# In what pieces the last output blocks of a gated MLP leave, and from which step

## The chip, the cores and the metric

The kernel runs on one core of a Trainium2 chip. The metric is the device time of one execution in microseconds (us). TensorE (PE) multiplies, ScalarE (ACT) and VectorE (DVE) take results out of PSUM, GpSimd (POOL) adds tiles and starts some transfers, and SyncE (SP) computes nothing: it starts DMA transfers. DMA transfers started by SP run on the queue that the profile calls q1, those started by ACT on q10; both are carried by the same 16 DMA engines.

## The reference

```python
# x: 16 x 256 x 512, w1: 512 x 4096, w2: 2048 x 512, all float32
h = x @ w1
gate, value = np.split(h, 2, axis=-1)
h = np.maximum(gate, 0) * value
return (h @ w2).astype(np.float32)
```

With the two leading axes of `x` taken together there are 4096 rows of 512.

## The kernel before

The rows are worked on in four sets (`s` = 0 to 3) of 1024. Both products are computed by a scheme of Strassen's kind: each is cut into 2 x 2 quarters, and seven products, `P1` to `P7`, of sums of quarters take the place of eight. The inputs are cast to float16; sums collect in float32 in PSUM.

The first product of a set runs in 16 blocks of 128 hidden columns (`class Block`). The second product of a set is a generator, `mm2_stream(s, go)`. Its matmuls are slipped in, four at a time, between those of the next set's first product, so that TensorE always has work; the last set's stream (`last`, `s` = 3) has nothing to hide behind and runs alone at the end of the program.

Within `mm2_stream` an output block `b` (0 to 3) stands for 128 rows of the set's upper half and 128 of the lower. Each of the seven products of a block is a chain of eight matmuls (`mm`, L288 to L293; the profile's L291), and each has its own evacuation in `step`:

- `P2`: ACT writes the left half of the upper output tile `o1` (L315).
- `P3`: DVE writes the right half of `o1` (L321), and SP sends `o1` to DRAM (L324). In the last set the blocks with `b` >= 1 go as two halves of 256 columns, 128 KB each; all others go whole, 256 KB.
- `P7`: DVE writes the right half of the lower output tile `o2` (L327). In the last set SP sends this half at once for the last block, `b` = 3 (L330).
- `P4`: ACT writes the left half of `o2` (L333). For `b` = 3 of the last set ACT itself sends this half (L335, on its own queue). In every other case SP sends the whole `o2` (L337).

`o2` is a part of the buffer named `pv`, so in the profile `out_dram<-pv` are the lower blocks and `out_dram<-o` the upper ones.

The order of the steps is written out by hand (`order`, L340 to L343). It ends with P6 of b=2 and 3, P3 of b=2 and 3, P7 of b=2 and 3, P4 of b=2 and 3. Every engine runs its instructions in the order in which they are recorded, so SP's last transfers before the change are: `o1` of b=2 in two halves, `o1` of b=3 in two halves, the right half of `o2` of b=3 (L330), the whole `o2` of b=2 (L337). Then come the program's branch (L45: the results of a test of the inputs decide whether a general way must be run as well; it is not run here) and the closing semaphore instructions (the launch line, L648), in which SP waits for every transfer that is still out.

A transfer that SP or ACT starts also waits until the transfer eight places before it, on the same semaphore, has landed.

Of the kernel before, what the change touches and what calls it, by code (L numbers as in the profile page):

```python
# [25 lines left out]
HALF = 256  # L26
# [3 lines left out]
@with_exitstack  # L30
def kernel(ctx: ExitStack, tc: tile.TileContext, x, w1, w2, out):

    nc = tc.nc
    x2 = x.flatten_outer_dims()
    out2 = out.flatten_outer_dims()  # L40
    flagpool = ctx.enter_context(tc.tile_pool(name="flagpool", bufs=1))
    flag = flagpool.tile([1, 1], dt.int32, name="flag")
    with ExitStack() as fast:
        unfit = fast_way(fast, tc, x2, w1, w2, out2, flag)
    with tc.If(unfit > 0, label="general"):  # L45
        with ExitStack() as general:
            general_way(general, tc, x2, w1, w2, out2)
# [52 lines left out]
def fast_way(ctx, tc, x2, w1, w2, out2, flag):  # L100

    nc = tc.nc
    T, D = x2.shape
    _, J = w1.shape
    H, DO = w2.shape
# [4 lines left out]
    NB = TH // P  # L110
# [11 lines left out]
    w1_v = w1.rearrange("(e p) (g j) -> p e g j", p=P, g=2)  # L122
    w2_v = w2.rearrange("(hc p) n -> p hc n", p=P)
    x_v = x2.rearrange("(s b p) d -> s p b d", p=P, b=2 * NB)
    out_v = out2.rearrange("(s h b p) n -> s h b p n", p=P, b=NB, h=2)
# [43 lines left out]
    gate = wpool.tile([P, 1], F32, name="gate")  # L169

    first = wpool.tile([P, 4], F32, name="first")
    nc.scalar.dma_start(out=first[:128], in_=w1_v[:128, :, 0, 0])

    def idle(n):
        for _ in range(n):
# [108 lines left out]
    def mm2_stream(s, go):  # L284
        last = s == NS - 1
        S = {}

        def mm(name, b, ps, fresh):  # L288
            vn, gn = WX[name]
            for k in range(NHC):  # L290
                nc.tensor.matmul(ps, go[gn][:, k, b * P:(b + 1) * P], V[vn][:, k, :], start=fresh and k == 0,  # L291
                                 stop=k == NHC - 1, skip_group_check=True)
                if k < NHC - 1:  # L293
                    yield

        def take(pool, nm):
            return pool.tile([P, TH], F32, name=nm, tag=nm)[:, :HALF]

        def step(name, b):
            d = S.setdefault(b, {})  # L300
            if name == "P1":
                d["X"] = take(psx, "X")
                yield from mm("P1", b, d["X"], True)
                d["Y"] = take(psy, "Y")
                nc.scalar.copy(out=d["Y"], in_=d["X"])
            elif name == "P5":
                d["W"] = take(psw, "W")
                yield from mm("P5", b, d["W"], True)
                t = tmp.tile([P, 2, TH], F32, name="pv", tag="tmp")
                d["pu"], d["o2"] = t[:, 0].rearrange("p (a n) -> p a n", a=2), t[:, 1]  # L310
                nc.scalar.activation(d["pu"][:, 0], d["W"], COPY, scale=1 / GS)
            elif name == "P2":
                yield from mm("P2", b, d["X"], False)
                d["o1"] = tmp.tile([P, DO], F32, name="o", tag="o", bufs=4)
                nc.scalar.activation(d["o1"][:, :HALF], d["X"], COPY, scale=1 / GS)  # L315
            elif name == "P6":
                yield from mm("P6", b, d["Y"], False)
                nc.scalar.activation(d["pu"][:, 1], d["Y"], COPY, scale=-1 / GS)
            elif name == "P3":
                yield from mm("P3", b, d["W"], False)  # L320
                nc.vector.scalar_tensor_tensor(out=d["o1"][:, HALF:], in0=d["W"], scalar=1 / GS, in1=d["pu"][:, 1],  # L321
                                               op0=MULT, op1=ADD)
                for n in (slice(0, HALF), slice(HALF, DO)) if last and b else (slice(0, DO),):
                    nc.sync.dma_start(out=out_v[s, 0, b, :, n], in_=d["o1"][:, n])  # L324
            elif name == "P7":
                yield from mm("P7", b, d["Y"], False)
                nc.vector.scalar_tensor_tensor(out=d["o2"][:, HALF:], in0=d["Y"], scalar=-1 / GS, in1=d["pu"][:, 0],  # L327
                                               op0=MULT, op1=ADD)
                if last and b == NB - 1:
                    nc.sync.dma_start(out=out_v[s, 1, b, :, HALF:], in_=d["o2"][:, HALF:])  # L330
            else:
                yield from mm("P4", b, d["Y"], False)
                nc.scalar.activation(d["o2"][:, :HALF], d["Y"], COPY, scale=1 / GS)  # L333
                if last and b == NB - 1:
                    nc.scalar.dma_start(out=out_v[s, 1, b, :, :HALF], in_=d["o2"][:, :HALF])  # L335
                else:
                    nc.sync.dma_start(out=out_v[s, 1, b], in_=d["o2"])  # L337
            yield

        order = [("P1", 0), ("P1", 1), ("P1", 2), ("P2", 0), ("P2", 1), ("P2", 2)]  # L340
        order += [(n, b) for n in ("P5", "P6", "P3", "P7", "P4") for b in (0, 1)]
        order += [("P1", 3), ("P5", 2), ("P2", 3), ("P5", 3)]
        order += [(n, b) for n in ("P6", "P3", "P7", "P4") for b in (2, 3)]  # L343
        for i, (n, b) in enumerate(order):
            for f in BESIDE.get((s, i), ()):
                f()
            yield from step(n, b)
# [190 lines left out]
    for s in range(NS):  # L538
        if s:
            g, go = g_tiles()  # L540
        first = NPLAIN if s == 0 else 0
# [4 lines left out]
        last = NJ * PERIOD  # L546
# [16 lines left out]
        for at in range(first * PERIOD, last + PERIOD):  # L563
            if at in plan:
                jb, n = plan[at]
# [87 lines left out]
```

## Time and profile before

| | us |
|---|---|
| median of 4 runs (309.27 to 309.72) | 309.66 |
| the profiled execution | 309.57 |
| its span, first to last instruction | 307.8 |
| PE busy | 300.1 |
| DVE busy | 219.3 |
| ACT busy | 189.7 |
| last ACT evacuation (L333, b=3) starts, ends | 303.00, 303.38 |
| last transfer (L335) is started | 303.42 |

The granted TensorE clock is 0.997 over the span. The page's row of HBM traffic:

```profile
HBM read 24.12 MB, written 11.53 MB: 116 GB/s over the span
```

How to read the views used below. The page gives the busy time of each engine and the chain of work that ended last. A timeline row gives start, duration, engine, source line, operation, the tile written and the tiles read; `SPq` and `ACTq` are the instructions with which SP and ACT start a transfer, and their duration is that of the start alone. The DMA view counts, for a stretch of time, the packets and megabytes of each DMA queue and the time their packets took as a share of 16 engines: 100% would be all sixteen engines moving that queue's packets for the whole stretch. A 256 KB output of 128 rows is 128 packets of 2 KB, eight on each engine, and 16 more of a few bytes that mark completion, one on each engine; a half block is 128 packets of 1 KB and the 16 marks. Queues with the kind "instruction" carry the engines' own program.

### The profile page before, as it was taken

To read this page: it belongs to the slowest core of one execution; us is meant where nothing else is said; L and a number is where in the kernel's file an instruction comes from. 1 tells how busy PE (TensorE), PEld (TensorE's weight loads), DVE (VectorE), ACT (ScalarE), POOL (GpSimd) and SP (SyncE) were. 2 spreads that over 40 slices of the span, in tenths; PEclk is the share of its full clock that TensorE was granted. 3 is DMA by queue.
4 is the path that set the end of the run, shared out by engine and by line. 5 is a ranking of instruction groups with operands and counts; after the bars stand their busy time and mean duration, and the time that the engine had idled before them with its cause. 6 is when DMAs were issued, how large, how long until landed. Compare 5 with 4: busy or idle time off the path is not lost.

```text
span 307.8 us, 5116 instructions
## 1 busy us (share of the span) xinstructions
PE 300.1 (97%) x1868; PEld 181.9 (59%) x1868; DVE 219.3 (71%) x346; ACT 189.7 (62%) x457; POOL 139.7 (45%) x127
## 2 busy tenths in 40 slices
PE   7899999999999999999999999999999999999993
PEld 3574444588844444488864444458884444448883
DVE  1798898896468888884338888886526888888311
ACT  2557776568577676738766767656856767673230
POOL 1749999810004438980002245994000343998000
PEclk9999999999999999999999999999999999999998
DMA  6999986989615740064130010037321100000223
GB/s 225 306 204 205 209 209 181 187 151 196 230 58 102 139 102 1 2 129 146 70 137 27 8 34 2 0 69 140 140 91 45 34 11 25 0 2 0 70 90 120
DMA packets 34410, 31.54 MB, mean 102 GB/s; under 512 B 14448, under 2 KB 28784, under 8 KB 34160
## 3 DMA queue, kind: packets, MB, share of 16 engines
q1 hardware_dynamic: 24608, 20.32, 21.8%
q0 software_dynamic: 9104, 10.75, 21.2%
q8 instruction: 15, 0.25, 0.3%
q10 hardware_dynamic: 672, 0.13, 0.2%
q14 instruction: 11, 0.09, 0.1%
HBM read 24.12 MB, written 11.53 MB: 116 GB/s over the span
## 4 chain that ended last, share of the span: by engine, by line
PE 95%; DMA 2%; ACT 0%; SPq 0%; issue 0%; ACTq 0%
PE Y L205 26%; PE X L205 17%; PE W L205 17%; PE Y L291 14%; PE W L291 9%; PE X L291 9%; DMA g<-in_w_dram 2%; PE W L255 2%; PE X L255 1%; PE Y L255 1%; SPq L418 0%; PE X L390 0%; ACT Y L212 0%; ACT wr L400 0%; ACT pv L333 0%
## 5 line engine op out<-in xcount | busy, mean ns | idle before, releaser
L280 POOL TENSOR_TENSOR g_S<-g 128x512 f16<-128x512 f16 (+1 forms) x46 | 58.1, 1292 | 126.2 <-DVE g L244 126.2
L205 PEld LDWEIGHTS <-wt 128*128 128x128 f16 x488 | 47.7, 98 | 55.9 <-issue 0.3
L205 PE MATMUL X<-x_A,wr 128*128 128x512 f16 x244 | 72.6, 379 | 0.1
L205 PE MATMUL Y<-x_S,wt 128*128 128x512 f16 x244 | 72.6, 379 | 0.0
L205 PEld LDWEIGHTS <-wr 128*128 128x128 f16 x366 | 35.8, 98 | 41.5 <-issue 0.4
L232 DVE SCALAR_TENSOR_TENSOR cc<-W,pu 128x512 f32<-128x512 f32 x61 | 42.2, 692 | 24.1 <-ACT pu L226 24.1
L212 ACT COPY Y<-X 128x512 f32<-128x512 f32 x61 | 34.8, 570 | 38.0 <-PE X L205 37.6
L291 PEld LDWEIGHTS <-g_S 128*128 128x128 f16 x512 | 50.0, 98 | 5.8
L238 DVE SCALAR_TENSOR_TENSOR cc<-Y,pu 128x512 f32<-128x512 f32 x61 | 42.2, 691 | 6.3
L226 ACT ACTIVATE pu<-Y 128x512 f32<-128x512 f32 x61 | 36.4, 596 | 13.9 <-PE Y L205 13.9
L233 DVE SCALAR_TENSOR_TENSOR g<-X,cc 128x512 f16<-128x512 f32 x61 | 42.2, 692 | 2.4
L244 DVE SCALAR_TENSOR_TENSOR g<-Y,cc 128x512 f16<-128x512 f32 x61 | 41.6, 681 | 1.8 <-PE Y L205 1.8
L291 PEld LDWEIGHTS <-g 128*128 128x128 f16 x384 | 37.5, 98 | 8.2
L219 ACT ACTIVATE pu<-W 128x512 f32<-128x512 f32 x61 | 36.8, 603 | 0.3 <-PE W L205 0.3
L205 PE MATMUL W<-x_S,wt 128*128 128x512 f16 x122 | 36.3, 379 | 0.0
L205 PE MATMUL W<-x_S,wr 128*128 128x512 f16 x122 | 36.3, 379 | 0.0
L205 PE MATMUL Y<-x_A,wt 128*128 128x512 f16 x122 | 36.3, 379 | 0.0
L291 PE MATMUL X<-w,g 128*128 128x256 f16 x256 | 31.2, 273 | 0.0
L291 PE MATMUL Y<-v,g_S 128*128 128x256 f16 x256 | 30.6, 273 | 0.0
L321 DVE SCALAR_TENSOR_TENSOR o<-W,pv 128x256 f32<-128x256 f32 x16 | 6.8, 424 | 29.8 <-PE W L291 29.8
L280 POOL TENSOR_TENSOR g_S<-g,g_S 128x512 f16<-128x512 f16 x18 | 21.8, 1209 | 1.4
L280 POOL TENSOR_TENSOR g_S<-g_S,g 128x512 f16<-128x512 f16 x18 | 20.8, 1155 | 1.4
(76 smaller groups left out, 284.6 us busy)
## 6 DMA issues: line engine op xcount, KB each, us to landing
out_dram<-pv SPq DMA_DIRECT2D x15, 256.0 KB, 2.0
out_dram<-o SPq DMA_DIRECT2D x13, 256.0 KB, 2.1
x<-in_x_dram POOLq DMA_DIRECT2D x3, 1024.0 KB, 8.1
xn<-x SPq DMA_DIRECT2D x12, 256.0 KB, 3.2
g_S<-in_x_dram SPq DMA_DIRECT2D x4, 512.0 KB, 6.5
wr<-in_w_dram POOLq DMA_DIRECT2D x4, 512.0 KB, 12.9
w<-in_w_dram POOLq DMA_DIRECT2D x4, 512.0 KB, 15.2
g<-in_w_dram SPq DMA_DIRECT2D x2, 512.0 KB, 6.6
```

What stands on the lines that cost most here:

```text
L205: nc.tensor.matmul(ps, W(wn, self.jb)[:, b], self.xo[xn][:, b, :], start=fresh and b == 0, stop=b == 1, skip_group_check=True)
L212: nc.scalar.copy(out=self.Y, in_=self.X)
L219: nc.scalar.activation(self.p5, self.W, COPY, scale=GS)
L226: nc.scalar.activation(self.u2, self.Y, COPY, scale=-GS)
L232: nc.vector.scalar_tensor_tensor(out=self.c12, in0=self.W, scalar=GS, in1=self.u2, op0=MULT, op1=ADD)
L233: nc.vector.scalar_tensor_tensor(out=self.g[:, self.jb, :TH], in0=self.X, scalar=0.0, in1=self.c12, op0=MAX, op1=MULT)
L238: nc.vector.scalar_tensor_tensor(out=self.c22, in0=self.Y, scalar=-GS, in1=self.p5, op0=MULT, op1=ADD)
L244: nc.vector.scalar_tensor_tensor(out=self.g[:, self.jb, TH:], in0=self.Y, scalar=0.0, in1=self.c22, op0=MAX, op1=MULT)
L255: nc.tensor.matmul(ps[:, ts], W(names[e // 2], self.jb)[:, e % 2], self.a[:, e, ts], start=e == 0, stop=e == 3, skip_group_check=True)
L280: eng.tensor_tensor(go[n][:, h0:h1], go[i0][:, h0:h1], go[i1][:, h0:h1], op=op)
L291: nc.tensor.matmul(ps, go[gn][:, k, b * P:(b + 1) * P], V[vn][:, k, :], start=fresh and k == 0, stop=k == NHC - 1, skip_group_check=True)
L321: nc.vector.scalar_tensor_tensor(out=d["o1"][:, HALF:], in0=d["W"], scalar=1 / GS, in1=d["pu"][:, 1], op0=MULT, op1=ADD)
```

## The change

For the last set only, the blocks are cut at other places:

- upper blocks (`P3`, L324): b=1 goes whole instead of in two halves; b=2 and b=3 go in halves as before.
- lower blocks: for b=2 too the right half is sent behind P7 (L330), and behind P4 only the left half is sent, 128 KB instead of 256 KB, still by SP. b=3 is as before.
- the load of one column of `w1` into `first` is written without the slice `:128`; the tile has 128 rows.

The count of transfers stays the same: one fewer for `o1` of b=1, one more for `o2` of b=2. SP's last transfers are now: `o1` of b=2 in two halves, `o1` of b=3 in two halves, the right half of `o2` of b=2, the right half of `o2` of b=3, the left half of `o2` of b=2. The instructions of PE, DVE, ACT and POOL are the same, in the same order.

```diff
-    nc.scalar.dma_start(out=first[:128], in_=w1_v[:128, :, 0, 0])
+    nc.scalar.dma_start(out=first, in_=w1_v[:, :, 0, 0])
...
-                for n in (slice(0, HALF), slice(HALF, DO)) if last and b else (slice(0, DO),):
+                for n in (slice(0, HALF), slice(HALF, DO)) if last and b >= 2 else (slice(0, DO),):
                     nc.sync.dma_start(out=out_v[s, 0, b, :, n], in_=d["o1"][:, n])
...
-                if last and b == NB - 1:
+                if last and b >= NB - 2:
                     nc.sync.dma_start(out=out_v[s, 1, b, :, HALF:], in_=d["o2"][:, HALF:])
...
                 if last and b == NB - 1:
                     nc.scalar.dma_start(out=out_v[s, 1, b, :, :HALF], in_=d["o2"][:, :HALF])
                 else:
-                    nc.sync.dma_start(out=out_v[s, 1, b], in_=d["o2"])
+                    n = slice(0, HALF if last and b == NB - 2 else DO)
+                    nc.sync.dma_start(out=out_v[s, 1, b, :, n], in_=d["o2"][:, n])
```

## The prediction

> **What bounds the kernel now.** I read the page first, then the chain of waits at the end, the timeline of the last microseconds, and the DMA view in narrow windows. The page says that TensorE is the whole kernel:
>
> ```profile
> PE 300.1 (97%) x1868; PEld 181.9 (59%) x1868; DVE 219.3 (71%) x346; ACT 189.7 (62%) x457; POOL 139.7 (45%) x127
> PE 95%; DMA 2%; ACT 0%; SPq 0%; issue 0%; ACTq 0%
> ```
>
> PE is busy for 300.1 of 307.8 us. The edit touches no matmul, and no DVE or ACT operation, so the only time it can change is the stretch behind the last matmul. The timeline of that stretch:
>
> ```profile
> 300.39 0.42 DVE L327 SCALAR_TENSOR_TENSOR pv<-Y,pv 128x256 f32<-128x256 f32 x1 [0.39 <-PE Y L291]
> 301.26 0.42 DVE L327 SCALAR_TENSOR_TENSOR pv<-Y,pv 128x256 f32<-128x256 f32 x1 [0.45 <-PE Y L291]
> 301.71 0.33 SPq L330 DMA_DIRECT2D out_dram<-pv  x1
> 302.13 0.38 ACT L333 ACTIVATE pv<-Y 128x256 f32<-128x256 f32 x1 [3.98 <-PE Y L291]
> 302.54 0.33 SPq L337 DMA_DIRECT2D out_dram<-pv  x1
> 303.00 0.38 ACT L333 ACTIVATE pv<-Y 128x256 f32<-128x256 f32 x1 [0.49 <-PE Y L291]
> 303.42 0.38 ACTq L335 DMA_DIRECT2D out_dram<-pv  x1
> ```
>
> The two DVE rows are P7 of b=2 and of b=3. L330 sends the right half of b=3, L337 the whole of b=2 (256 KB), L335 the left half of b=3 (128 KB). In the DMA views the times from issue to landing are 2.5 us for L330, 3.2 for L337 and 2.7 for L335, so they land at 304.2, 305.7 and 306.1. The span ends at 307.8: some 1.7 us of closing semaphore instructions (L648) that start when L335 has landed. So **the landing of L335 sets the end**, and its issue, behind the last ACT copy, is not moved by the edit. It takes 2.7 us, where the other 128 KB outputs of the page take 1.8 (median of six). The edit can only win from the 0.9 us between.
>
> What holds L335 back shows in three windows of the DMA view: 303.0 to 304.25, 304.65 to 305.26, and 305.26 to 305.62.
>
> ```profile
> q8 instruction: 1, 0.02, 6.1%
> ...
> q10 hardware_dynamic: 41, 0.03, 14.7%
> q1 hardware_dynamic: 6, 0.01, 6.5%
> ...
> q10 hardware_dynamic: 9, 0.01, 6.5%
> q1 hardware_dynamic: 1, 0.00, 0.2%
> ```
>
> q1 is SP's queue and q10 ACT's. In the first window one single packet of instructions (0.02 MB) takes 6.1% of 16 engines over 1.25 us: 0.061 x 16 x 1.25 = 1.22 us on one DMA engine, from 303.0 to 304.2. In the second window L337 still has six packets to go, and in the third, behind the very last packet of q1 (its completion mark), come exactly nine packets of q10: 144 packets / 16 engines = 9, one engine's whole share of L335 (eight of data and the mark). So one DMA engine, call it X, was held by the instruction load to 304.2, then moved its eight 2 KB packets of L337 until 305.26, and only then began its share of L335, until 305.62; 0.5 us later that is seen as landed.
>
> **The change, part by part.**
>
> The load of `first` (L172) is written differently and is the same transfer: 0. So is the slice of L337 for every other block.
>
> P3 of b=1: its two halves (L324) become one transfer. SP loses one DMA and one wait. The three issues of L324 (b=0, then the two halves of b=1) stand in the timeline from 288.47 to 289.79, so the right half goes out at about 289.4, and with it now the whole. SP next stands still at L337 of b=0 until 292.1, and nothing reads an output. Even at 5.1 us, the longest landing of any output, it is down by 294.5, 11 us before the end: 0, hidden by 13 us of matmuls.
>
> P7 of b=2: SP gains one DMA, L330 for b=2. DVE is done at 300.39 + 0.42 = 300.81; SP starts L330 0.03 us after DVE, as it does for b=3 (301.68 to 301.71), so at 300.84, and is free at 301.17. Behind it in SP's queue stand L330 of b=3, which cannot go before 301.71, and the send of b=2 behind P4, not before 302.54: 0.54 us of slack, then 0.50. Cost on the path: 0. Its packets should run some 0.83 us after the start of the issue (L330 now: 301.71, first packets at 302.54), so from 301.67 to 302.2. That stretch is empty now: the window from 301.5 to 302.45 shows no packet at all.
>
> P4 of b=2: 128 KB instead of 256 KB leave at 302.54. This is the part that can gain. On engine X eight packets of 1 KB take the place of eight of 2 KB. Two rows price it.
>
> ```profile
> q1 hardware_dynamic: 145, 0.26, 74.5%
> ...
> q1 hardware_dynamic: 432, 0.39, 73.9%
> ...
> q1 hardware_dynamic: 9, 0.01, 6.9%
> ```
>
> First, the plain pace. The window 292.8 to 293.75 holds one 256 KB output: 0.745 x 16 x 0.95 / 128 = 0.088 us per 2 KB packet. The window 299.9 to 301.5 holds three of 128 KB: 0.739 x 16 x 1.6 / 384 = 0.049 us per 1 KB packet. Eight of each: 0.71 against 0.39, a gain of 0.31. Second, a like case: an instruction load of the same 0.02 MB at 290.6 leaves one engine working alone on 1 KB packets, and in the window from 291.745 to 292.466 that engine moves exactly eight of them and a mark, in 0.72 us. L337's share took 305.26 - 304.22 = 1.04 us. Gain 1.04 - 0.72 = 0.32. I take **0.32**, the second, because it has the load in front of it as the path does. Bounds: 0 below (the load, or another engine, holds L335 whatever L337 weighs), 0.9 above (L335 lands in the undisturbed 1.8 us).
>
> A rule speaks against counting on this. The Trainium skill, "Runtime: NRT & Kernel Launch", section "Instruction fetch mechanics", says that instructions come in blocks of 16 KiB and that a taken branch out of the window forces such a load. The load on q8 agrees with it in size, but the other queue of instructions, q14, shows 0.01 MB and 5.6% of 16 engines over the 0.65 us from 304.05, which is 0.58 us. With a full block there (an estimate, 1.2 us as on q8) it would run to 305.3 and L335 behind it to 305.7, so no gain, 309.6; by the row it is gone at 304.7.
>
> The sum is made against the profiled execution: 309.57 (span 307.8 and 1.8 around it) - 0.32 = 309.25. That execution is 0.09 under the median of the runs, 309.66, which gives 309.34; I say **309.3**.
>
> **Rivals.**
>
> *Nothing moves (25%).* L335 is held by something else: the engine that is last but one. The window from 305.1 on shows ten packets of q10, X's nine and a single one more, so that engine ends some 0.5 us before X; if it too is held by an instruction load (q14 at 304.1, on an engine no view names), it may slip later. For it: two loads fall into this stretch. Against: nine q10 packets stand in a row behind q1's last mark. Time 309.6.
>
> *L335 lands undisturbed (12%).* Its landing falls from 2.7 to 1.8 us: 309.57 - 0.9 = 308.7. For it: with half the bytes the other fifteen engines are free before L335 comes. Against: the load on q8 follows TensorE's branch (L45 at 301.8), which the edit does not move, so X is still taken until 304.2 and owes 0.72 + 0.39 us of work after that.
>
> *Slower, through SP's queue (8%).* The added L330 stands in front of L330 of b=3 and of the P4 send. Issues are 0.33 us as a rule, but the longest L324 took 1.06. Two such: 300.84 + 2.12 = 302.96 instead of 302.54, so the P4 send and SP's own branch come 0.42 us late. It decides once the two issues together take over 1.70 us. The price: SP's instruction load then comes at 304.5 instead of 304.1, and on X it would stand before L335: 305.62 - 0.32 + 0.58 = 305.88, 0.26 over now: 309.8. Against: from 150 us on no output's issue on SP takes over 0.40.
>
> **How the numbers follow.** 55% for the forecast. The range, 308.9 to 309.8, holds the forecast, no movement and the third rival at its price, over eight in ten; the undisturbed landing lies outside. A difference under 0.2% (0.62 us) cannot be told from no change here, and 0.32 us is half of that. Faster by more needs a landing gain of over 0.62 us: most of the second rival and a little of the forecast's tail, 0.15. Slower by more would need over twice the third rival's price: 0.05. The rest, 0.80.
>
> **What would show it.** L330 twice, at 300.8 and 301.7, each 0.33 us. Packets on q1 from about 301.7 to 302.2. The P4 send of b=2 at 302.5 landing in about 2.9 instead of 3.2 us, L335 in about 2.4. The last q10 packet at about 305.3 instead of 305.6, and the closing instructions still 1.7 us. PE busy as before, 300 us. Wrong it would be if L335 still takes 2.7 us (another holder), if it takes 1.8, or if the closing stretch behind the last landing changes length.

## The result, and the profile after

| | runs | median us | range | 
|---|---|---|---|
| before | 78 | 309.80 | 309.12 to 311.51 |
| changed | 52 | 309.34 | 308.79 to 311.98 |

The ratio is 0.9981, with a 95% interval of 0.9972 to 0.9990: some 0.6 us faster by the ratio, 0.46 us by the medians, just at the border of what this kernel can show.

The profiled execution of the changed kernel, though, is a late one: 310.83 us, with a span of 308.9 us against 307.8. So the two traces must be compared stretch by stretch. First the page, span and engines:

```profile
span 308.9 us, 5116 instructions
PE 302.3 (98%) x1868; PEld 184.0 (60%) x1868; DVE 219.4 (71%) x346; ACT 189.5 (61%) x457; POOL 139.6 (45%) x127
```

PE is busy for 2.2 us more, with the same 1868 matmuls. Where that came from shows at the very start. Here is PE's timeline of the changed kernel, and then that of the kernel before (start, duration, what):

```profile
1.28 3.59 PE L177 MATMUL Y<-warm 128*128 128x512 f16 x8 [1.28 <-DVE warm L167]
5.58 1.94 PE L383 MATMUL W<-ident,g_S 128*128 128x128 f32 x8 [0.70 <-DMA g_S<-in_x_dram]
```

```profile
1.28 3.60 PE L177 MATMUL Y<-warm 128*128 128x512 f16 x8 [1.28 <-DVE warm L167]
5.51 1.06 PE L382 MATMUL W<-ident,g_S 128*128 128x128 f32 x8 [0.64 <-DMA g_S<-in_x_dram]
```

The eight warming matmuls are alike, but the first eight transposes, the same work, take 1.94 us instead of 1.06. The trace's record of the granted clock begins its stretch at full speed at 10.28 us in the changed kernel and at 5.47 in the kernel before. From some 14 us on each matmul runs 1.45 us later. Of what the edit touches only the load of `first` has run by then; its issue takes 476 ns from 0.8 us on in both traces, and it lands after 4.3 us before and 4.4 now. This is a lottery of the first microseconds that both kernels play (below).

What the edit does lies at the other end. The timeline there, of SP and of ACT:

```profile
302.29 1.21 SPq L330 DMA_DIRECT2D out_dram<-pv  x2
303.99 0.33 SPq L338 DMA_DIRECT2D out_dram<-pv  x1
...
303.58 0.38 ACT L333 ACTIVATE pv<-Y 128x256 f32<-128x256 f32 x1 [3.98 <-PE Y L291]
304.45 0.38 ACT L333 ACTIVATE pv<-Y 128x256 f32<-128x256 f32 x1 [0.49 <-PE Y L291]
304.87 0.38 ACTq L335 DMA_DIRECT2D out_dram<-pv  x1
```

L330 now stands there twice (the first at 302.29, less the 1.45 us at 300.84, as forecast), and L338 is the send behind P4. To take out the late start I count from the start of the last ACT evacuation: 303.00 before, 304.45 now. To the span's end it was 4.78 us and is 4.48: **0.30 us shorter**. L335 lands 2.4 us after its issue instead of 2.7; here are its rows in the DMA views, before and now:

```profile
out_dram<-pv ACTq DMA_DIRECT2D x1, 128.0 KB, 2.7
out_dram<-pv ACTq DMA_DIRECT2D x1, 128.0 KB, 2.4
```

The DMA view shows how, in three windows: 304.44 to 305.70, 305.68 to 306.418 and 306.415 to 306.8.

```profile
q8 instruction: 1, 0.02, 6.1%
...
q1 hardware_dynamic: 9, 0.01, 6.9%
...
q10 hardware_dynamic: 9, 0.01, 6.1%
```

The instruction load on q8 ends at 305.69 (0.061 x 16 x 1.26 = 1.23 us long, as before). Then the engine that it held moves L338's eight 1 KB packets and the mark, until 306.41: 0.72 us, where eight of 2 KB took 1.04. Last come the nine packets of q10, its share of L335, until 306.76.

### The profile page after: what moved, and what is told of

Its sections match the earlier page's. It is cut to its first block, busy times and chain, and to the rows that moved or that the text cites. A ratio compares the mean times of both kernels' runs of the same rounds, so it can differ in the third digit from the quotient of the medians.

```text
span 308.9 us, 5116 instructions
## 1 busy us (share of the span) xinstructions
PE 302.3 (98%) x1868; PEld 184.0 (60%) x1868; DVE 219.4 (71%) x346; ACT 189.5 (61%) x457; POOL 139.6 (45%) x127
## 4 chain that ended last, share of the span: by engine, by line
PE 96%; DMA 1%; ACT 0%; issue 0%; SPq 0%; ACTq 0%
PE Y L205 25%; PE X L205 17%; PE W L205 17%; PE Y L291 14%; PE X L291 9%; PE W L291 9%; PE W L255 2%; DMA g_S<-in_x_dram 1%; PE X L255 1%; PE W L383 1%; PE Y L255 1%; PE X L383 1%; PE X L391 0%; ACT Y L212 0%; PE Y L177 0%
```

## The experiments

Each run's trace gives the same few marks. They are read from its DMA and instruction records, in us from the start of the last ACT evacuation (L333): when the load on q8 ends, when q1's last packet ends, the difference of these two, when q10's last packet ends, when L335 has landed, when the span ends, and the closing stretch, which is the last minus the one before it (taken before rounding).

| kernel | KB behind P4 | load ends | q1 ends | difference | q10 ends | L335 landed | span ends | closing |
|---|---|---|---|---|---|---|---|---|
| before | 256 | 1.23 | 2.27 | 1.04 | 2.61 | 3.07 | 4.78 | 1.70 |
| changed | 128 | 1.24 | 1.96 | 0.72 | 2.31 | 2.78 | 4.48 | 1.70 |
| e1 P7, P4 part alone | 128 | 1.35 | 2.08 | 0.72 | 2.42 | 2.89 | 5.64 | 2.75 |
| e2 P3 part alone | 256 | 1.22 | 2.26 | 1.03 | 2.60 | 3.06 | 4.84 | 1.77 |
| e3 right half twice | 256 | 0.88 | 1.92 | 1.04 | 2.26 | 2.72 | 4.43 | 1.70 |
| e4 left half unsent | 0 | 0.87 | | | 1.81 | 2.16 | 3.93 | 1.77 |
| e5 no general way | 128 | no load | 0.89 | | 1.79 | 2.14 | 3.10 | 0.96 |
| e6 late branch | 128 | 3.15 | 1.00 | | 3.87 | 4.36 | 6.06 | 1.70 |
| e7 nine warming | 128 | 1.08 | 1.80 | 0.72 | 2.15 | 2.62 | 4.32 | 1.70 |
| e8 four warming | 128 | 0.85 | 1.58 | 0.72 | 2.00 | 2.46 | 4.16 | 1.70 |
| e10 b=0 in halves | 256 | 1.08 | 2.12 | 1.03 | 2.46 | 2.92 | 5.68 | 2.75 |
| e11 b=2 whole | 128 | 0.99 | 1.70 | 0.71 | 2.04 | 2.51 | 4.71 | 2.20 |
| e12 before, nine | 256 | 0.99 | 2.02 | 1.03 | 2.37 | 2.83 | 4.53 | 1.70 |
| e13 changed, nine | 128 | 1.00 | 1.72 | 0.72 | 2.06 | 2.54 | 4.24 | 1.70 |

### e1 and e2: one part of the change at a time

```diff
 e1, against the changed kernel
-    if last and b >= 2 else (slice(0, DO),):      # L323, P3
+    if last and b else (slice(0, DO),):
 e2, against the kernel before
-    if last and b else (slice(0, DO),):           # L323, P3
+    if last and b >= 2 else (slice(0, DO),):
```

> The change without its P3 part: b=1 of the upper blocks goes in two halves again, only the P7 and P4 sends of b=2 are changed. Theory (the gain is the halved send of b=2 behind P4, on the one DMA engine that the instruction load of TensorE holds): the stretch from the start of the last ACT evacuation to the span's end is as in the changed kernel, 4.48 us (before: 4.78), and L335 takes 2.4 us to land; time some 0.3 us under the kernel before. Rival (the whole block of b=1 does it): the stretch is 4.78 and L335 takes 2.7.

> Of the change only the P3 part: b=1 of the upper blocks goes whole, the lower block of b=2 goes whole behind P4 as before. Theory: nothing moves, last stretch 4.78 us, L335 takes 2.7 us, the same time as the kernel before within 0.1%. Rival: the stretch is 4.48 and 0.3 us are won.

e1: 310.28 us median against 309.83 of the kernel before beside it, ratio 1.0018 [0.9994, 1.0042]. e2: 309.98, ratio 0.9996 [0.9972, 1.0021]. e2 came as expected but for 0.07 us in the closing stretch. e1 is a miss: L335 lands as the theory wants (2.5 us, with a load that took 1.37 us instead of 1.23), but the span ends 5.64 us after the last evacuation began, not 4.48. **The split alone makes the kernel slower**; the P3 part, priced at nothing, is what saves it. The interval of all the times still takes in 1, because late starts widen both groups; the trace shows it (5.64 us against 4.78 before), and among the runs under 310.5 us, which I take to be the early starts, e1 has a median of 310.22 and the kernel before beside it 309.74.

What SP waits for at the end shows the reason. The view of SP's waits gives who waited for whom, total us, times, longest. First the changed kernel, then e1:

```profile
SPq L45 <- SPq L45: 2.5, 4, 1.5
```

```profile
SPq L45 <- SPq L45: 2.9, 1, 2.9
```

And the rows of L45 and of L649's drains by source line (durations least, median, most in ns; first and last start), again the changed kernel and then e1:

```profile
L45 SPq EVENT_SEMAPHORE  x8: 17/17/17, 304.9 to 307.2; - x8
...
L649 SPq DRAIN  x3: 7/13/36, 308.1 to 308.6; - x3
```

```profile
L45 SPq EVENT_SEMAPHORE  x8: 17/17/17, 305.8 to 306.4; - x8
...
L649 SPq DRAIN  x3: 7/7/136, 307.6 to 308.0; - x3
```

Behind its branch, and under the branch's line L45, SP waits for the eight DMA semaphores one after the other, in the same order in every trace that has the branch. In the changed kernel it passes six early, stands 1.5 us at the seventh (L338), and the last of the eight is L335's: the others lie in the shadow of the landings. In e1 there is one transfer more, and since transfers take the eight semaphores in turn, L335 gets the next one round, the *first* that SP asks for. SP stands there for 2.9 us, and seven more waits follow behind the landing, from 305.82 to 306.37: 0.54 us. (e2 fits: with one transfer fewer L335 falls on the seventh, one wait is left behind it, and the closing stretch is 0.07 us longer.) A second piece lies inside L649, and the view of waits has no row for it. By the start times in the instruction records SP stands for 0.36 us in front of its first drain, where the changed kernel has 0.04, and the drain takes 136 ns instead of 13; with three waits before it that came a little slower, L649 takes 2.13 us from its first instruction to the span's end instead of 1.62, 0.51 us more. 0.54 + 0.51 is the 1.05 us by which the closing stretch grew.

### e10 and e11: the count of transfers, without the split and with it

```diff
 e10, against the kernel before
-    if last and b else (slice(0, DO),):           # P3
+    if last else (slice(0, DO),):
 e11, against the changed kernel
-    if last and b >= 2 else (slice(0, DO),):      # P3
+    if last and b % 2 else (slice(0, DO),):
```

> The kernel before with b=0 of the upper blocks in halves too: one more transfer of 128 KB, at about 288 us, 15 us before the end, and nothing else. In the kernel without the P3 part the eight closing waits of SP (L45) all came after L335 had landed, since L335 then uses the semaphore that SP waits for first, and the closing stretch behind its landing grew from 1.70 to 2.75 us. Theory (the number of transfers decides which of eight semaphores L335 uses, and so whether SP's other closing waits lie in its shadow): the closing stretch behind the landing is 2.7 us here too, the whole stretch from the last ACT evacuation about 5.8 us, the time about 1.0 us over the kernel before. Rival (it was the early send of b=2): as the kernel before, 1.71 and 4.78 us.

> The changed kernel with another upper block left whole: b=1 goes in halves again and b=2 whole, so that the number of transfers is that of the changed kernel. Theory (the P3 part is there to keep the count, whichever block pays): closing stretch 1.70 us, the stretch from the last ACT evacuation 4.1 to 4.6 us according to how long TensorE's instruction load takes, the time as the changed kernel. Rival (b=1 itself must go whole): closing stretch 2.7 us, 1 us slower.

e10: 310.65 us against 309.74, ratio 1.0042 [1.0025, 1.0059]; closing stretch 2.75 us. One more transfer of a block that left 15 us before the end costs 0.9 us, with nothing of the split in it (4.78 to 5.68 us; the load happened to be 0.15 us shorter). That is shown as the theory said.

e11: 309.94 us, ratio 1.0010 [0.9996, 1.0024]; closing stretch 2.20 us. This is half a miss, and a useful one. The count of transfers is that of the changed kernel and L335 is again on the semaphore asked for last, so the 0.54 us of waits are gone. But the other 0.5 us is still there: L649 again takes 2.12 us to the span's end instead of 1.62. SP stands for 0.37 us in front of its second drain, and that drain is a long one:

```profile
L649 SPq DRAIN  x3: 7/13/131, 306.5 to 307.2; - x3
```

So it is a cost of its own. It goes with how many *instructions* SP has run. A transfer that waits for two things needs an instruction more than one that waits for one; the left half of b=2, which SP sends by itself in the changed kernel, needed only the one, and in e11 it goes with the whole block. Counted in the traces, SP runs 150 instructions in both kernels, 152 in e1 and e10 and 151 in e11, and in these three the stop comes at the 148th each time (the first closing drain in e1 and e10, the second in e11). In the kernels with 150 the 148th is a wait for GpSimd: in the changed kernel SP passes it 0.22 us behind ACT, but GpSimd is still clearing semaphores then and the end is no later for it. In e2 and e4, with 148, it is the last instruction of all. That SP fetches its next block of program there is my reading of a place that stays fixed while instructions move past it. The DMA records speak for it: the last 8 KB load on q14, one of the queues that carry program, begins 0.64 to 0.65 us behind the start of the 148th instruction in eleven of the thirteen traces with the branch (0.57 in e2, 0.71 in e6), wherever that instruction stands. But it begins when the stop is over, so it is not what SP stood for, and what was is not shown.

### e3 and e4: the bytes behind P4

```diff
 e3, against the changed kernel
+                elif last and b == NB - 2:
+                    spare = dpool.tile([P, DO], F32, name="spare")
+                    nc.sync.dma_start(out=spare[:, HALF:], in_=d["o2"][:, HALF:])
...
-                    n = slice(0, HALF if last and b == NB - 2 else DO)
+                    n = slice(0, DO)
 e4, against the changed kernel
-                else:
+                elif not (last and b == NB - 2):
```

> The changed kernel, but the early right half of b=2 goes to a spare buffer in DRAM, and behind P4 the whole block of b=2 goes, 256 KB. The same number of transfers behind P7, the old bytes behind P4. Theory (bytes in front of L335 decide): stretch back at 4.78 us, L335 2.7 us, the send behind P4 3.2 us. Rival (what counts is that something leaves early, or the order of the transfers): 4.48 us and 2.4.

> The changed kernel without the send of the left half of b=2 behind P4: that half block is left out of the output. Theory: the held engine has nothing in front of its share of L335 but the instruction load, so it begins when the load ends (1.25 us after the start of the last ACT evacuation) and moves its eight packets in 0.72 us; L335 lands 2.0 us after its issue, stretch about 4.1 us. Rival (another engine, the last but one, holds L335 next): L335 still lands at 1.9 to 2.4 us and the stretch stays between 4.1 and 4.48.

e3: 309.49 us against 309.83, ratio 0.9982 [0.9965, 0.9999]; 4.43 us. By its time this is a miss: as fast as the changed kernel, with the old bytes behind P4. By the trace the bytes do what the theory says and something else moved. The load on q8, in the window from 304.43 to 305.33:

```profile
q8 instruction: 1, 0.02, 6.1%
```

That is 0.061 x 16 x 0.90 = 0.88 us instead of 1.23, and behind it the 2 KB packets took 1.04 us, as in every trace with 256 KB. With a load of 1.22 us, as before, its 4.43 would be 4.77 (an estimate). Whether this program's load is short in all its runs or was so in the profiled one cannot be told from the times alone, so e3 by itself does not decide; the table's column of differences does. It reads 1.03 or 1.04 in all five traces with 256 KB and 0.71 or 0.72 in all six with 128 KB where the load stands in front, whenever the load ended (0.85 to 1.35 us).

e4, which leaves that half block out of the output: 308.86 us, ratio 0.9961 [0.9943, 0.9980]; 3.93 us, where 4.1 was expected, again with a load of only 0.88 us; it ends before L335's data come out, and L335 lands in 1.7 us, as undisturbed. The closing stretch is 1.77 us, as in e2: here too there is one transfer fewer.

### e5 and e6: the load itself

```diff
 e5, against the changed kernel
-    with tc.If(unfit > 0, label="general"):
-        with ExitStack() as general:
-            general_way(general, tc, x2, w1, w2, out2)
...
-    BESIDE[NS - 1, 20] = [lambda: tc.mark_branch_hint_location(
-        "general", engines=[ENG.PE, ENG.SP, ENG.Activation, ENG.DVE, ENG.Pool])]
 e6, against the changed kernel, behind L335's line
+                    nc.tensor.matmul(take(psw, "W")[:1, :1], d["o2"][:, :1], d["o2"][:, :1], start=True, stop=True)
```

> The changed kernel without the general way and the branch to it (the fast way's result and its test of the inputs are as before; the way for unfit inputs is left out). Theory: without the branch no engine loads instructions from a far place at the end, so no packet on q8 or q14 in the last 5 us, no engine is held, L335 lands in the undisturbed 1.8 us, and the stretch behind the start of the last ACT evacuation is some 0.6 us shorter than in the changed kernel, 3.9 us. Rival (L335 is slow because of what runs on q1 in front of it, loads or not): L335 still takes 2.4 us and the stretch stays at 4.48 less what the branch itself costs.

> The changed kernel with one more matmul of 1 x 1 at the very end that reads what the last ACT evacuation wrote; TensorE so reaches its branch about 1.6 us later (303.4 in place of 301.8 on the clock of the kernel before). Theory: the load on q8 starts 1.25 us after that branch, so some 0.35 us after the first packets of L335, when most of them are through; the engine that it holds has moved its share, L335 lands in 1.9 to 2.0 us, the stretch is about 4.05 us, 0.4 us under the changed kernel. Rival (the load is not what holds L335): 4.48 us, or longer by the matmul.

e5: 307.62 us, ratio 0.9908 [0.9873, 0.9943]; 3.10 us. The DMA view from 301 to the end has no queue of instructions left:

```profile
q1 hardware_dynamic: 568, 0.52, 30.0%
q10 hardware_dynamic: 144, 0.13, 7.6%
...
out_dram<-pv ACTq DMA_DIRECT2D x1, 128.0 KB, 1.7
```

L335 lands in 1.7 us; together with e4 that says that the loads are what held it: 0.64 us of the 1.38 by which e5's stretch is shorter. The rest, 0.74 us, is closing stretch (0.96 instead of 1.70), which the theory had not counted. It is no version to use, since unfit inputs would get a wrong result.

e6: 310.93 us, ratio 1.0037 [1.0013, 1.0061]; 6.06 us. A miss, and my mechanism for the load's timing falls with it. TensorE's branch came 1.68 us later, as meant, and of the loads behind the branches only that on q8 came later with it, so it is TensorE's. But it did not start 1.25 us behind it, where L335 would mostly have been through; it started 1.84 us behind it, at 305.18, and L335 was *not* through. In the windows from 305.18 to 306.06 and from 306.04 to 306.8:

```profile
q8 instruction: 1, 0.02, 6.2%
...
q10 hardware_dynamic: 9, 0.01, 6.7%
```

A whole engine's share of L335, nine packets, moved only behind the load, though the other fifteen engines were done with theirs some 0.3 us before the load's packet begins, and from 304.92 to 305.18 no packet moved at all. So the engine is taken for longer than the load's own packet shows. Why, and from when, stays open. The order is the same as before the edit: load first, outputs behind it.

### e7, e8, e12 and e13: the start

```diff
 e7 and e13, against the changed kernel; e12, against the kernel before
-NWARM = 8
+NWARM = 9
 e8, against the changed kernel
-NWARM = 8
+NWARM = 4
```

> The changed kernel with nine warming matmuls instead of eight at the start, so that TensorE idles some 0.2 us instead of 0.6 to 0.7 before the first transposes. In the profile of the changed kernel the granted clock reaches full speed only at 10.28 us, in that of the kernel before at 5.47, and everything up to the last set lies 1.45 us later. Theory (the clock's rise is decided by how long TensorE idled in the first microseconds, and the two groups of times, near 309.4 and near 311, are the two cases): the group near 311 vanishes, all times lie under 309.9, the median is some 0.3 us lower or the same. Rival (the late rise has another cause): the group stays at a sixth to a third of the runs.

> The changed kernel with four warming matmuls instead of eight: TensorE idles some 2.3 us before the first transposes. Theory (as for nine): every run has the late rise of the clock, all times near 310.8 to 311.3, and the profile shows full speed after 8 us. Rival (the first set's start does not depend on the warming): two groups as in the changed kernel, median near 309.4.

> The kernel before with nine warming matmuls. Theory: no run with the late rise of the clock, so all times between 309.1 and 310.1, median about 309.6.

> The changed kernel with nine warming matmuls, beside the kernel before with nine on the same chip: the change's own size without the lottery of the first microseconds. Theory: 0.3 us under that kernel, median about 309.25, all times under 309.9. Rival (part of the measured gain was that fewer of its runs began late): the two are within 0.1 us.

| kernel | warming matmuls | runs | over 310.5 us | median us | ratio to before |
|---|---|---|---|---|---|
| before (with the changed kernel) | 8 | 78 | 23 | 309.80 | |
| changed | 8 | 52 | 5 | 309.34 | 0.9981 [0.9972, 0.9990] |
| e8 changed | 4 | 10 | 7, all over 310.3 | 310.89 | 1.0017 [0.9997, 1.0038] |
| e7 changed | 9 | 12 | 0 | 309.24 | 0.9975 [0.9958, 0.9992] |
| e12 before | 9 | 12 | 0 | 309.50 | 0.9996 [0.9985, 1.0006] |
| e13 changed | 9 | 12 | 0 | 309.25 | 0.9977 [0.9963, 0.9990] |

With four, the first eight transposes take 1.94 us again and the clock's record reaches full speed at 9.52 us. With nine no run of 36 was late. The theory's result holds, its mechanism does not quite: in e7's trace TensorE still idles 0.73 us before the first transposes, since the clock had already risen at 4.2 us and the nine matmuls took only 3.54.

```profile
1.28 3.54 PE L177 MATMUL Y<-warm 128*128 128x512 f16 x9 [1.28 <-DVE warm L167]
5.55 1.06 PE L383 MATMUL W<-ident,g_S 128*128 128x128 f32 x8 [0.73 <-DMA g_S<-in_x_dram]
```

So it is not that gap. What the runs show is the amount of warming: with four matmuls all runs took over 310.3 us, with eight some took over 310.5, with nine none did. Single times went outside what was expected all the same: 310.12 and 310.27 in e12, 310.13 in e13, and four runs of e8 between 310.31 and 310.55. e12 and e13, on one chip and without the lottery, give the edit's own size: 309.50 to 309.25, 0.25 us (with twelve runs each, uncertain by some 0.2 us), and 0.29 us between their traces (4.53 to 4.24). e13 and e7 are one kernel on two chips; its medians are the lowest, 0.9977 and 0.9975 of the kernel before, but these intervals overlap that of the changed kernel.

## Why the prediction was right, and where it was wrong by its own steps

- **The end is set by L335's landing and a closing stretch of 1.7 us.** Right in these two kernels (1.70 in both). That the 1.7 us is fixed was wrong: it depends on the semaphore that L335 falls on and on SP's count of instructions, from 1.70 to 2.75 us in these runs, and it is 0.96 without the branch.
- **One DMA engine, held by TensorE's instruction load, moves L338's share first and L335's last.** Right: nine packets of q10 in a row at the end, and the same order in every trace where a load stands before them. Without loads (e5) L335 lands in 1.7 us. What the prediction did not know is that the load's length varies, from 0.88 to 1.37 us in these traces; that it was 1.22 and 1.23 us in the two that it compares was luck.
- **The term of 0.32 us (1.04 to 0.72).** Measured 1.04 to 0.72, and 0.30 in the stretch to the span's end. The plain pace of packets would have given 0.31, but the like case was the better guide: behind a load, eight 1 KB packets take 0.72 us, not 0.39.
- **"P7 of b=2 ... Cost on the path: 0" and "0, hidden by 13 us of matmuls" for P3 of b=1.** These are the steps that failed, and they failed against each other. One transfer more costs 1.05 us at the very end (e1, e10), 0.54 us through the order of the waits and 0.51 us through the stop at SP's 148th instruction, far from where it is issued; leaving b=1 whole gives it back. The sum of zero was right only because the change does both. I had followed what each transfer waits for and what waits for its data, and not that SP closes by asking for eight semaphores in a fixed order, each of which goes to every eighth transfer. Had the change come without its P3 part, my forecast would have been over 0.7 us off. (A slip beside it: 294.5 is 13.3 us before the end of the span, not 11; nothing hangs on that.)
- **The rule on instruction blocks, weighed against the row.** The row was right: the load on q14 behind SP's branch took 0.51 us (0.01 MB), and the gain stayed.
- **Rivals.** Nothing moves: the last but one engine ended its share of L335 at 1.8 to 2.1 us in these traces, before the last one in all of them (2.12 against 2.61 before, 1.91 against 2.31 now), and held nothing in the two kernels. Undisturbed landing: needs the loads gone, as e5 shows. Slower through SP's queue: the issues of L330 took 0.33 us, so it never came near. The way in which the split really can be slower, through the closing waits, was not among them.
- **The size by the runs.** 309.34 against a forecast of 309.3; but part of the 0.46 us between the medians is that 23 of 78 runs of the kernel before took over 310.5 us and only 5 of 52 of the changed one, which I read as late starts, and that is luck. The runs under 310.5 us have medians of 309.68 and 309.29, 0.39 us apart. The cleanest readings of the edit's own part are 0.29 and 0.30 us between pairs of traces, and 0.25 us from e12 to e13.

## What to carry to other kernels

Before a transfer is split or merged, count how many transfers follow in the program: where semaphores go round in turn and the closing code asks for them in a fixed order, the one that lands last should fall on the one asked for last (here nothing lost; 0.07 us on the seventh, 0.54 on the first). At the end of a program the engines' own instruction loads share the DMA engines with the last outputs, so what matters there is the bytes that stand between such a load and the last transfer on one engine, not the mean load of all sixteen. And when two profiles differ at the start, line them up at the last common event before reading the end.

## What the runs showed of the hardware

- The same load of 0.02 MB took from 0.88 to 1.37 us in the thirteen traces that have it at the end of the program. In the eleven with an output of 128 or 256 KB behind it on the same engine, that output's last packet comes a fixed time after the load's end (1.03 to 1.04 us with 256 KB, 0.71 to 0.72 with 128), so the end of the transfers moves with the load one for one.
- For some 0.6 us behind such a load the engine is slow: eight 1 KB packets took 0.72 us, where the plain pace is 0.39.
- SP needs 0.07 to 0.10 us for each closing wait whose semaphore has already come (seven of them in 0.54 us in e1).
- The clock of TensorE rises early (between 4.0 and 6.0 us in the traces at hand) or late (9.5 to 10.4), and late costs 1.45 us here. The Trainium skill, "TensorE: Matmul & The Clock Gate", Part 1, says that the window in which activity is judged is free-running, so that the moment of the rise varies with where in it the first matmul falls. The early rises agree with that in kind: they spread over 2 us, though the first matmul starts at 1.28 us in all traces but e5's (1.19). Its figure of about 3.4 us of sustained work does not foretell the odds: eight matmuls kept TensorE busy for at most 3.6 us, and 23 of 78 runs took over 310.5 us; nine kept it busy for at most 4.0 us, and none of 36 did. That those 23 are late rises is read from their times; only the profiled executions have a clock record.
